# Token-major norms of a two-block transformer kernel: transposes and splits of a token tile emitted one tile later, inverse root as one GpSimd power

## The chip, the cores and the metric

One Trainium2 chip, one core. The metric is the device time of one execution in microseconds (us), median of the runs shown. Engine names are those of the profile: PE (TensorE matmul), PEld (its weight load), DVE (VectorE), ACT (ScalarE), POOL (GpSimd), SP (the engine that issues most loads).

## The reference, cut to what matters

Two transformer blocks in float32 on 512 tokens of width 1024. The change touches only the places where a sum goes into the residual stream, is normalised there and is normalised again for the next matrix product. In the second block that is, for each of two layers and three sublayers (mixers, cross attention, MLP):

```python
x = x + rms_norm(merged @ w_mix_out[l], ln_mix_post[l])
h = rms_norm(x, ln_xa_pre[l])          # goes into the next projection
```

with `rms_norm(x, g) = x * rsqrt(mean(x * x) + 1e-6) * g` over the 1024 features of a token. The end of the first block has one such place with no sum in front (`rmsnorm(x, norm_final)`), and the last sublayer writes the output and has no second norm. So there are seven such places, of which six are followed by a further projection.

## The kernel before, in words

Matrix products run as three products each: a matrix is split in a high part (ACT copies it, rounding to a shorter format) and a low part (DVE takes the difference), and PE adds hi x hi, hi x lo and lo x hi (lines 370 to 372, and 946 to 948 in the token-major form). Weights come by DMA from SP into `wraw` (3 buffers), ACT makes `whi` (L360), DVE `wlo` (L361), 3 buffers each.

`post` (lines 973 to 1057) does one of the seven places. Its product is token-major: 128 tokens on the partitions, 1024 output features in two halves m = 0 and 1, four token tiles t = 0 to 3. `wide` (L950) runs one half: the first chunks of the weights for all four tiles, and then, tile by tile, the held chunks (three of them in the second half; two in the MLP, whose last group has only two), after which it calls `done(t)`. `done` scales the sum by the gain or adds it to what is there (DVE, L1002, L1004 or L1006) and lets ACT square it with a running sum (L1008). In the second half `done(t)` goes on to `norm(t)`:

- the inverse root on DVE, ten instructions of one column each: add the two halves and epsilon (L1015), three for the start value (L1016 to L1018), three Newton steps of two (L1020, L1021);
- the update of the residual x, 128x1024 (L1024; or L1026; or L1029 and L1030);
- if a projection follows, eight PE transposes of the new x into two PSUM buffers `pax` (L1038), eight splits of their 128 columns into `hhi` (ACT, L408) and `hlo` (DVE, L409), and two ACT squares of x for the next norm (L1043).

The ten small values stand in `tss`, one buffer. The scratch output of each ACT square is a buffer of tag `dt` (six buffers, used all over the kernel, also for `vm` below).

Behind the two halves come, in order of emission: `fill` (four of the six places: four 512 KB matrices of the memory's keys or values, split, multiplied with 256 memory rows into PSUM, scaled by DVE into `vm`, L903, transposed or not, and sent out by a DMA from the POOL queue), `hold` (the first three weight tiles of the next projection), and in the next function `lead`: three output tiles of the next projection, their 512 tokens in two halves of 256 columns, so that its first half needs only the splits of tiles 0 and 1 and its second half those of tiles 2 and 3.

Order: no instruction is placed by hand. A planner in the compiler takes, for each engine and by its own estimate of durations, the earliest emitted instruction that it holds to be ready, and so fixes a queue for each engine; on the chip an engine goes through its queue strictly in order and waits where the estimate was wrong.

Of the kernel before, what the change touches and what calls it, by code (L numbers as in the profile page):

```python
# [10 lines left out]
F32 = mybir.dt.float32  # L11
F32R = mybir.dt.float32r
I32 = mybir.dt.int32
AF = mybir.ActivationFunctionType
OP = mybir.AluOpType
AX = mybir.AxisListType

P = 128
# [55 lines left out]
class Packed:  # L74
    def __init__(self):
        self.parts, self.at, self.n = [], {}, 0
# [176 lines left out]
class Kern:  # L253
    def __init__(self, ctx, tc, a, vat):
        self.tc, self.nc, self.a, self.vat = tc, tc.nc, a, vat
        pool = lambda name, bufs, **k: ctx.enter_context(tc.tile_pool(name=name, bufs=bufs, **k))
        self.const = pool("const", 1)
        self.big = pool("big", 1)
        self.wp = pool("wp", 3)
        self.wk = pool("wk", 2)  # L260
        self.ps = pool("ps", 1, space=bass.MemoryType.PSUM)
        self.turn, self.dtags, self.led, self.held = 0, ("pmm", "pr"), [], []
        self.dram = pool("dram", 2, space=bass.MemoryType.DRAM)
        nc = self.nc
        self.x = self.bigt("x", F32, "rbig")
        self.cst = self.const.tile([P, _CONST.n], F32, name="cst")
        self.vec = self.const.tile([P, a["vec"].shape[1]], F32, name="vec")
        nv = vat["norm_mix0"][1]
        nc.scalar.dma_start(self.vec[:, :nv], a["vec"][:, :nv])
        one = self.const.tile([P, 1], F32, name="one")  # L270
        nc.vector.memset(one, 0.0)
        nc.scalar.activation(one, one, AF.Exp)
        first = self.leads("pool_in")
        raws = self.half("w01", F32).rearrange("p k t -> p (k t)").rearrange("p (c k m) -> p c k m", c=2, k=KD)
        raws = [raws[:, 0], raws[:, 1], self.wtile("wraw")]
        self.held = [(self.wtile("whi"), self.wtile("wlo")) for _ in range(3)]

        def xload(ks):
            for k in ks:
                nc.sync.dma_start(self.x[:, k], a["xT"][:, k])  # L280

        xload([0])
        for part, then in ((slice(0, 4), (1, 2, 3)), (slice(4, 8), (4, 5, 6, 7))):
            for raw, ap, (hi, lo) in zip(raws, first, self.held):
                nc.sync.dma_start(raw[:, part], ap[:, part])
                nc.scalar.activation(hi[:, part], raw[:, part], AF.Copy)
                nc.vector.tensor_sub(lo[:, part], raw[:, part], hi[:, part])
            xload(then)
        nc.sync.dma_start(self.cst, a["cst"])
        nc.sync.dma_start(self.vec[:, nv:], a["vec"][:, nv:])  # L290
        self.load_phase(_CONST1, a["cst1"])
        self.ident = self.c("ident")
        self.ones = self.c("ones")[:, 0:1]
        self.nsplit = 0
# [678 lines left out]
    def post(self, chunks, xh, xl, mode, y, gname, nxt, then=(), out=None, fill=None):  # L973

        nc = self.nc
        if fill:
            fill = self.mem_kv(*fill, ("pmm", "pr"))
        g = self.rows(gname)  # L980
        old, own = self.x, mode == "own"
        if own:
            self.x = self.bigt("x", F32, "rbig")
        x = self.x
        ss = self.wk.tile([P, 4, 8], F32, name="tss", bufs=1)
        z = [None]
        pn = None
        flat = lambda v, t: v[:, 2 * t:2 * t + 2].rearrange("p m t -> p (m t)")

        def residual(m):  # L990
            def add(t, ps):
                for j in range(4):
                    nc.tensor.matmul(ps[:, j * P:(j + 1) * P], old[:, 4 * m + j, t * P:(t + 1) * P], self.ident,
                                     start=False, stop=False)
            return add if own else None

        def half(m):
            def done(t, ps):
                i = 2 * t + m
                src = ps  # L1000
                if mode == "fresh":
                    nc.vector.tensor_mul(y[:, i], ps, g[:, m * T:(m + 1) * T])  # L1002
                elif own:
                    nc.vector.tensor_copy(x[:, i], ps)  # L1004
                else:
                    nc.vector.tensor_add(y[:, i], y[:, i], ps)  # L1006
                    src = y[:, i]
                nc.scalar.activation(self.dt("sq"), src, AF.Square, scale=1.0 / 32, accum_out=ss[:, t, m:m + 1])  # L1008
                if m:
                    norm(t)  # L1010
            return done

        def norm(t):
            v, i, r, h, w = (ss[:, t, j:j + 1] for j in range(2, 7))
            nc.vector.tensor_scalar(v, ss[:, t, 0:1], ss[:, t, 1:2], 1e-6, op0=OP.add, op1=OP.add)  # L1015
            nc.vector.tensor_scalar(i.bitcast(I32), v.bitcast(I32), 1, None, op0=OP.logical_shift_right)  # L1016
            nc.vector.tensor_scalar(r.bitcast(I32), i.bitcast(I32), -1.0, float(0x5F3759DF), op0=OP.mult, op1=OP.add)
            nc.vector.tensor_scalar(h, v, -0.5, None, op0=OP.mult)  # L1018
            for _ in range(3):
                nc.vector.scalar_tensor_tensor(w, r, h, r, op0=OP.mult, op1=OP.mult)  # L1020
                nc.vector.scalar_tensor_tensor(r, w, 1.5, r, op0=OP.add, op1=OP.mult)  # L1021
            xt = flat(x, t)
            if mode == "fresh":
                nc.vector.scalar_tensor_tensor(xt, flat(y, t), r, xt, op0=OP.mult, op1=OP.add)  # L1024
            elif own:
                nc.vector.scalar_tensor_tensor(xt, xt, r, g, op0=OP.mult, op1=OP.mult)  # L1026
            else:
                yt = flat(y, t)
                nc.vector.scalar_tensor_tensor(yt, yt, r, g, op0=OP.mult, op1=OP.mult)  # L1029
                nc.vector.tensor_add(xt, xt, yt)  # L1030
            if out is not None:
                nc.sync.dma_start(out[:, 2 * t:2 * t + 2], x[:, 2 * t:2 * t + 2])
                return
            c = slice(t * P, (t + 1) * P)
            for m in range(2):
                pt = self.pax()
                for j in range(4):
                    nc.tensor.transpose(pt[:, j * P:(j + 1) * P], x[:, 2 * t + m, j * P:(j + 1) * P], self.ident)  # L1038
                for j in range(4):
                    k = 4 * m + j  # L1040
                    self.split(pn["hi"][:, k, c], pn["lo"][:, k, c], pt[:, j * P:(j + 1) * P], scale=self.v(nxt, k))
            for m in range(2):
                nc.scalar.activation(self.dt("sq"), x[:, 2 * t + m], AF.Square, accum_out=sx[:, 2 * t + m:2 * t + m + 1])  # L1043

        sx = self.wk.tile([P, 8], F32, name="tsx", bufs=1)
        self.wide(chunks[0], xh, xl, 1, half(0), residual(0))
        if nxt:
            pn = {"hi": self.bigt("hhi"), "lo": self.bigt("hlo"), "g": nxt}
        self.wide(chunks[1], xh, xl, min(3, len(chunks[1])), half(1), residual(1))
        if fill:  # L1050
            fill()
        self.hold(then)
        if nxt:
            s4 = self.wk.tile([P, 4], F32, name="ts4", bufs=1)
            nc.vector.tensor_add(s4, sx[:, 0:8:2], sx[:, 1:8:2])
            pn["st"] = {"acc": [z, z], "ps": {0: s4, 1: s4}, "r": None}
        return pn
# [756 lines left out]
```

## Time and profile before

| what | us |
|---|---|
| median of 3 runs | 3443.78 |
| the 3 runs | 3444.88, 3434.6, 3443.78 |
| the profiled execution's own time | 3447.86 |
| its span | 3446.1 |
| PE busy in it | 3334.7 |
| DVE busy | 1833.2 |
| ACT busy | 1169.0 |
| POOL busy | 262.9 |

The span is the time from the first to the last instruction of the profiled execution. Granted clock is the share of TensorE's full clock that the chip let through, 0.983 over the whole execution. In the views of single instructions, `[6.89 <-DVE x L1030]` says that the engine stood idle for 6.89 us before the instruction and what ended the wait.

The seven places lie at about 1150 to 1210 us (end of the first block), 1740 to 1812 (mixers, layer 0), 1870 to 1952 (cross attention 0), 2240 to 2335 (MLP 0), 2880 to 2950 (mixers 1), 3030 to 3095 (cross attention 1) and 3380 to 3446 us (MLP 1, the output). The second, the third, the fourth and the fifth carry a `fill`.

### The profile page before, as it was taken

The numbers are of one execution on the slowest core, as the hardware profiler recorded it, in microseconds if no ns is written. First come the engines' busy times: TensorE is split into PE (matmuls) and PEld (weight loads), VectorE is DVE, ScalarE is ACT, GpSimd is POOL, SyncE is SP. The second block draws the span as 40 slices with busy tenths as digits, with TensorE's granted clock in tenths as the row PEclk, the third lists the DMA queues.
The fourth block names the chain that finished last, engine by engine and source line by source line (L and its number), as shares of the span: only waits on it lengthen the run. The fifth ranks groups of instructions, "written<-read, shape, count | busy, mean of one in ns | idle before, by whom it ended". The sixth has DMA issues, their size and how long they took to land.

```text
span 3446.1 us, 42433 instructions
## 1 busy us (share of the span) xinstructions
PE 3334.7 (97%) x16702; PEld 2704.5 (78%) x16702; DVE 1833.2 (53%) x3521; ACT 1169.0 (34%) x2076; POOL 262.9 (8%) x229
## 2 busy tenths in 40 slices
PE   7999999999999989999999999989999999899998
PEld 6888888878888867777887888877776788778886
DVE  7554444445545466556465644466565545454445
ACT  4332232543222333322343433343342234344232
POOL 3200022001000010001200000001100121000000
PEclk9999999989999999999999999989999999999999
DMA  3323335232232231232242322223222233213222
GB/s 134 107 95 97 100 121 159 80 130 101 98 98 92 92 100 44 69 108 90 92 141 80 123 98 98 96 90 109 57 56 93 80 98 122 99 56 109 98 96 76
DMA packets 96328, 334.16 MB, mean 97 GB/s; under 512 B 12472, under 2 KB 14016, under 8 KB 93824
## 3 DMA queue, kind: packets, MB, share of 16 engines
q1 hardware_dynamic: 88912, 295.64, 26.4%
q10 hardware_dynamic: 4528, 27.15, 2.2%
q0 software_dynamic: 2688, 8.66, 1.1%
q8 instruction: 131, 2.15, 0.3%
q14 instruction: 69, 0.57, 0.1%
HBM read 311.20 MB, written 13.90 MB: 94 GB/s over the span
## 4 chain that ended last, share of the span: by engine, by line
PE 66%; DVE 7%; ACT 2%; issue 1%; POOL 0%; DMA 0%; DVEq 0%; ACTq 0%; POOLq 0%
PE pmm L372 8%; PE pmm L371 7%; PE pmm L370 7%; PE pr L372 5%; PE pr L370 5%; PE pr L371 5%; PE pr L946 3%; PE pr L947 3%; PE pr L948 3%; PE pmm L947 3%; PE pmm L946 3%; PE pmm L948 3%; DVE wlo L361 1%; PE pax L1504 1%; PE pr L1722 1%
## 5 line engine op out<-in xcount | busy, mean ns | idle before, releaser
L360 ACT ACTIVATE whi<-wraw 128x1024 fp32r<-128x1024 f32 (+2 forms) x529 | 551.1, 1044 | 1624.0 <-PE pmm L371 532.4
L361 DVE TENSOR_TENSOR wlo<-wraw,whi 128x1024 fp32r<-128x1024 f32 (+2 forms) x529 | 648.9, 1228 | 321.2 <-ACT whi L360 317.1
L372 PE MATMUL pmm<-hhi,wlo 128*128 128x512 f32 (+1 forms) x1568 | 608.3, 388 | 9.0 <-DVE wlo L361 9.0
L370 PE MATMUL pmm<-hhi,whi 128*128 128x512 f32 (+1 forms) x1568 | 609.5, 389 | 6.6 <-ACT whi L360 6.0
L371 PE MATMUL pmm<-hlo,whi 128*128 128x512 f32 (+1 forms) x1568 | 609.9, 389 | 0.9 <-DVE hlo L409 0.9
L370 PE MATMUL pr<-hhi,whi 128*128 128x512 f32 (+1 forms) x1104 | 419.5, 380 | 10.8 <-ACT hhi L408 10.4
L372 PE MATMUL pr<-hhi,wlo 128*128 128x512 f32 (+1 forms) x1104 | 417.7, 379 | 2.8 <-DVE wlo L361 2.8
L371 PE MATMUL pr<-hlo,whi 128*128 128x512 f32 (+1 forms) x1104 | 418.0, 379 | 0.9 <-DVE hlo L409 0.8
L372 PEld LDWEIGHTS pmm<-hhi,wlo 128*128 128x128 f32 x1568 | 298.9, 191 | 69.2 <-DVE wlo L361 15.7
L370 PEld LDWEIGHTS pmm<-hhi,whi 128*128 128x128 f32 x1568 | 298.3, 190 | 66.1 <-ACT whi L360 10.4
L371 PEld LDWEIGHTS pmm<-hlo,whi 128*128 128x128 f32 x1568 | 298.3, 190 | 59.6 <-issue 4.4
L370 PEld LDWEIGHTS pr<-hhi,whi 128*128 128x128 f32 x1104 | 209.8, 190 | 51.1 <-ACT hhi L408 10.8
L372 PEld LDWEIGHTS pr<-hhi,wlo 128*128 128x128 f32 x1104 | 209.4, 190 | 43.9 <-DVE wlo L361 6.7
L371 PEld LDWEIGHTS pr<-hlo,whi 128*128 128x128 f32 x1104 | 209.9, 190 | 39.7 <-DVE hlo L409 2.0
L1630 POOL TENSOR_TENSOR macc<-macc,g 128x512 f32<-128x512 f32 x48 | 71.6, 1494 | 345.7 <-DVE g L1629 236.7
L582 DVE TENSOR_TENSOR u<-pmm,rstd 128x512 f32<-128x512 f32 x44 | 30.4, 691 | 108.6 <-PE pmm L372 102.9
L577 DVE TENSOR_TENSOR g<-pr,rstd 128x512 f32<-128x512 f32 x44 | 30.4, 691 | 90.4 <-PE pr L372 89.6
L1618 DVE TENSOR_TENSOR g<-pmm,rstd 128x512 f32<-128x512 f32 x44 | 30.3, 689 | 87.2 <-PE pmm L372 87.2
L948 PE MATMUL pr<-wlo,ahl 128*128 128x512 f32 x192 | 74.8, 390 | 0.0
L946 PE MATMUL pr<-whi,ahl 128*128 128x512 f32 x192 | 74.8, 389 | 0.0
L948 PE MATMUL pmm<-wlo,ahl 128*128 128x512 f32 x192 | 74.8, 389 | 0.0
L947 PE MATMUL pmm<-whi,ahl 128*128 128x512 f32 x192 | 74.7, 389 | 0.0
(553 smaller groups left out, 5644.8 us busy)
## 6 DMA issues: line engine op xcount, KB each, us to landing
wraw<-mlp SPq DMA_DIRECT2D x128, 512.0 KB, 3.3
wraw<-w_in SPq DMA_DIRECT2D x116, 512.0 KB, 3.3
wraw<-ffn_g SPq DMA_DIRECT2D x44, 512.0 KB, 3.3
wraw<-ffn_u SPq DMA_DIRECT2D x44, 512.0 KB, 3.3
wraw<-wkv SPq DMA_DIRECT2D x32, 512.0 KB, 3.3
wraw<-qkv SPq DMA_DIRECT2D x24, 512.0 KB, 3.6
wraw<-ffn_d SPq DMA_DIRECT2D x24, 448.0 KB, 3.3
wraw<-ffn_d SPq DMA_DIRECT2D x16, 512.0 KB, 3.5
```

The lines of the kernel that those rows point to most:

```text
L360: nc.scalar.activation(hi[:, :kt, :m], raw[:, :kt, :m], AF.Copy)
L361: nc.vector.tensor_sub(lo[:, :kt, :m], raw[:, :kt, :m], hi[:, :kt, :m])
L370: nc.tensor.matmul(ps[:, cols], hi[:, i], xh[:, k, cols], start=a, stop=False)
L371: nc.tensor.matmul(ps[:, cols], hi[:, i], xl[:, k, cols], start=False, stop=False)
L372: nc.tensor.matmul(ps[:, cols], lo[:, i], xh[:, k, cols], start=False, stop=z)
L577: nc.vector.tensor_mul(g, pg, r)
L946: nc.tensor.matmul(ps, xh[:, k, c], hi[:, m], start=a, stop=False)
L947: nc.tensor.matmul(ps, xl[:, k, c], hi[:, m], start=False, stop=False)
L948: nc.tensor.matmul(ps, xh[:, k, c], lo[:, m], start=False, stop=z)
L1504: nc.tensor.matmul(poA[:, oc], eT[:, b * P:(b + 1) * P], vn[:, b * P + 64 * br:b * P + 64 * br + 64], start=b == 0, stop=b == qb)
L1630: nc.gpsimd.tensor_add(acc[:, n], acc[:, n], g)
L1722: nc.tensor.matmul(po, V[:, b, n * P:(n + 1) * P], eT[b], start=b == 0, stop=b == 1)
```

## The change

The norm is cut into `update(t)` and `feed(t)`. `feed(t - 1)`, the transposes, splits and squares, is emitted behind `update(t)`, and `feed(3)` behind `fill`. The ten DVE instructions of the inverse root go; in their place POOL adds epsilon to the first half's sum (in the first half, off the norm's chain), and then, per tile, adds the second half's sum and raises it to the power -0.5, which it reads from a one-column constant.

```diff
+        self.neghalf = self.const.tile([P, 1], F32, name="neghalf")
+        nc.vector.memset(self.neghalf, -0.5)
...
                 nc.scalar.activation(self.dt("sq"), src, AF.Square, scale=1.0 / 32, accum_out=ss[:, t, m:m + 1])
-                if m:
-                    norm(t)
+                if not m:
+                    nc.gpsimd.tensor_scalar(ss[:, t, 2:3], ss[:, t, 0:1], 1e-6, None, op0=OP.add)
+                    return
+                update(t)
+                if nxt and t:
+                    feed(t - 1)
             return done
 
-        def norm(t):
-            v, i, r, h, w = (ss[:, t, j:j + 1] for j in range(2, 7))
-            nc.vector.tensor_scalar(v, ss[:, t, 0:1], ss[:, t, 1:2], 1e-6, op0=OP.add, op1=OP.add)
-            nc.vector.tensor_scalar(i.bitcast(I32), v.bitcast(I32), 1, None, op0=OP.logical_shift_right)
-            nc.vector.tensor_scalar(r.bitcast(I32), i.bitcast(I32), -1.0, float(0x5F3759DF), op0=OP.mult, op1=OP.add)
-            nc.vector.tensor_scalar(h, v, -0.5, None, op0=OP.mult)
-            for _ in range(3):
-                nc.vector.scalar_tensor_tensor(w, r, h, r, op0=OP.mult, op1=OP.mult)
-                nc.vector.scalar_tensor_tensor(r, w, 1.5, r, op0=OP.add, op1=OP.mult)
+        def update(t):
+            r = ss[:, t, 3:4]
+            nc.gpsimd.tensor_add(ss[:, t, 4:5], ss[:, t, 1:2], ss[:, t, 2:3])
+            nc.gpsimd.tensor_tensor(r, ss[:, t, 4:5], self.neghalf, op=OP.pow)
             xt = flat(x, t)
...
             if out is not None:
                 nc.sync.dma_start(out[:, 2 * t:2 * t + 2], x[:, 2 * t:2 * t + 2])
-                return
+
+        def feed(t):
             c = slice(t * P, (t + 1) * P)
...
         if fill:
             fill()
+        if nxt:
+            feed(3)
         self.hold(then)
```

## Rows read from the trace of the kernel before

**Rows 1.** The page, busy time: engine, us (share of the span), weight loads, instructions.

```profile
PE 3334.7 (97%) x16702; PEld 2704.5 (78%) x16702; DVE 1833.2 (53%) x3521; ACT 1169.0 (34%) x2076; POOL 262.9 (8%) x229
```

**Rows 2.** Who PE waited for, whole span: us in total, times, longest.

```profile
PE pax L1038 <- DVE x L1024: 13.0, 5, 6.0
PE pmm L372 <- DVE wlo L361: 12.2, 14, 2.3
...
PE pax L1038 <- DVE x L1030: 8.9, 3, 6.9
...
PE pax L1038 <- DVE z L1104: 3.0, 1, 3.0
PE pr L370 <- ACT sq L1008: 2.6, 2, 1.4
```

**Rows 3.** Busy by stretch: PE, PEld, DVE, ACT, POOL, granted clock, DMA, GB/s.

```profile
1190.00:1210.00 20.00, 15.84 (x108) 14.57 (x106) 15.09 (x56) 11.07 (x33) 0.00 (x0) 0.91 0.50 185
1795.00:1810.00 15.00, 12.23 (x89) 10.61 (x88) 10.63 (x31) 8.98 (x27) 1.31 (x3) 1.00 0.55 195
1940.00:1950.00 10.00, 7.69 (x57) 6.67 (x56) 9.28 (x30) 7.74 (x25) 1.29 (x3) 1.00 0.32 102
2295.00:2335.00 40.00, 28.26 (x164) 25.23 (x163) 30.01 (x91) 21.50 (x61) 2.06 (x3) 0.74 0.41 148
2925.00:2950.00 25.00, 15.80 (x108) 14.50 (x107) 18.09 (x62) 13.95 (x37) 2.00 (x3) 0.80 0.40 134
3075.00:3095.00 20.00, 16.13 (x115) 15.20 (x115) 14.20 (x58) 10.14 (x31) 0.00 (x0) 0.91 0.26 80
3430.00:3446.00 16.00, 1.87 (x9) 1.22 (x7) 11.84 (x38) 1.45 (x4) 0.00 (x0) 0.63 0.32 132
```

**Rows 4.** Single instructions of MLP 0, tiles 2 and 3: start, length, engine, line.

```profile
2297.22 0.68 DVE L1006 TENSOR_TENSOR ybm<-ybm,pr 128x512 f32<-128x512 f32 x1
...
2306.91 0.39 PE L370 MATMUL pmm<-hhi,whi 128*128 128x256 f32 x1
...
2314.18 0.63 ACT L1043 ACTIVATE sq<-x 128x512 f32<-128x512 f32 x1 [3.32 <-DVE x L1030]
...
2316.73 0.63 ACT L1008 ACTIVATE sq<-ybm 128x512 f32<-128x512 f32 x1
...
2321.78 1.22 DVE L1030 TENSOR_TENSOR x<-x,ybm 128x1024 f32<-128x1024 f32 x1
2322.92 0.41 DVE L903 TENSOR_TENSOR vm<-pmm,mr 128x256 f32<-128x256 f32 x1
...
2323.06 1.97 PE L1038 MATMUL pax<-cst,x 128*128 128x128 f32 x8 [6.89 <-DVE x L1030]
```

**Rows 5.** Single instructions of mixers 0, tile 0, from sum to transposes.

```profile
1774.38 0.21 DVE L1015 TENSOR_SCALAR tss<-tss 128x1 f32<-128x1 f32 x1 [0.75 <-ACT sq L1008]
...
1776.35 1.28 DVE L1024 SCALAR_TENSOR_TENSOR x<-yb,tss,x 128x1024 f32<-128x1024 f32 x1
...
1777.69 1.09 PE L1038 MATMUL pax<-cst,x 128*128 128x128 f32 x8
```

**Rows 6.** Single lines on POOL: duration in ns, least/median/most, first and last start; one memset.

```profile
L1513 POOL TENSOR_TENSOR oC<-oC,tA x8: 728/738/1252, 1332.3 to 2579.4; 128x256 f32<-128x256 f32 x8
L1630 POOL TENSOR_TENSOR macc<-macc,g x48: 1269/1293/2366, 1550.1 to 2878.7; 128x512 f32<-128x512 f32 x48
L1805 POOL MEMSET const-float32-0.0<- 128x1 f32 x1 | 0.1, 103 | 0.2 <-issue 0.2
```

**Rows 7.** The end: the last matmul and the last update.

```profile
3431.48 0.39 PE L948 MATMUL pmm<-wlo,ahl 128*128 128x512 f32 x1
...
3440.90 1.22 DVE L1030 TENSOR_TENSOR x<-x,ybm 128x1024 f32<-128x1024 f32 x1
```

**Rows 8.** Two stretches of unbroken matmuls, of 512 and of 256 columns (columns as rows 3).

```profile
1910.00:1915.00 5.00, 5.00 (x24) 4.14 (x23) 1.92 (x2) 1.08 (x2) 0.00 (x0) 1.00 0.31 105
1815.00:1820.00 5.00, 5.00 (x44) 5.00 (x43) 0.00 (x0) 0.00 (x0) 0.00 (x0) 1.00 0.00 1
```

## The prediction

> **What bounds the kernel now.** The first view is the page's busy time: PE is busy for 3334.7 of 3446.1 us [rows 1], so the end is set by PE and no cut on another engine counts unless it takes away PE's idle time, which is 111.4 us in all. The second is the list of waits of PE: its largest single cause is the transposes L1038 waiting for the residual x: 13.0 us on L1024, 8.9 on L1030, and 3.0 put down to a DVE memset that stands behind the last x update of the first block [rows 2]. That is 24.9 us in nine waits. The third is busy time by stretch around the six places that feed a projection [rows 3]. Length minus PE busy is 4.16, 2.77, 2.31, 11.74, 9.20 and 3.87 us: 34.05 us idle. The granted clock falls there as well, to 0.91, 0.74, 0.80 and 0.91 on average in four of the six. I estimate what that costs as (1 - clock) x PE busy: 1.4 + 7.3 + 3.2 + 1.5 = 13.4 us. So the change can touch some 47 us on PE, and besides that the tail, in which PE is done at 3431.9 and the core needs 14.2 us more [rows 7].
>
> Why x comes late is in the view of single instructions. In MLP 0 the sum of tile 3 is complete at 2297.9 (L1006), but its square on ACT (L1008) starts at 2316.7, 18.8 us later; it stands in ACT's queue behind both L1043 squares of tile 2, which had to wait for tile 2's x [rows 4]. So the tiles go one behind the other: x of a tile, its squares, only then the sum of squares of the next. DVE takes the first `vm` of the fill (L903) only at 2322.9, directly behind tile 3's x, and PE stood idle for 6.89 us until then [rows 4]. Both fit the order of emission: in the old code the squares of x(t) come ahead of the square of tile t+1, and tile 3's ahead of all `vm`, and they all draw on the six `dt` buffers. The planner does move work (the lead's L370 runs at 2306.9, ahead of the transposes of tile 2 that were emitted before it), but it did not move these.
>
> **The change part by part.**
>
> *Emission one tile later.* L1008 of tile t+1 now stands ahead of the squares, transposes and splits of tile t, so the tiles' updates no longer wait for each other's feed; the fill's `vm` stands ahead of feed(3). No instruction is added or removed here: 192 transposes, 192 pairs of splits and 48 squares remain. Their cover: a tile's held chunks are 18 matmuls, at 5.00/24 = 0.21 us each 3.8 us [rows 8]. From the last matmul of tile t, x needs 0.69 + 0.8 (sum, square and its read-out), the root, and 1.28 us for L1024 [rows 5]; with a root of 1 us this is 3.8 us, just under the next tile's held chunks. For tile 3 nothing of its own product follows, but the first half of the lead does, 3 tiles x 8 x 3 = 72 matmuls of 256 columns at 5.00/44 = 0.114 us, or 8.2 us [rows 8], and with a fill another four matrices of 24 such, 10.9 us. The cover is there in all six places. What is late next: in MLP 0 the held chunks are 12 matmuls (2.5 us) and the update is two instructions (L1029, L1030), so DVE is the tighter engine: it is busy for 30.0 of 40 us in that stretch [rows 3], and `wlo` of the fill queues on DVE behind a denser burst of updates. Waits for `wlo` are already 12.2 us over the kernel [rows 2]; I leave this part in. Ends: all 34.05 us of idle goes, or none. I take three quarters, as the 24.9 us of L1038 waits are 73% of it: -25.5 us.
>
> *Clock.* The slow stretches follow the long waits (MLP 0, mixers 1) and go with them. Ends 0 and -13.4; three quarters: -10 us.
>
> *Root on POOL.* Ten DVE instructions per tile go, 1.97 us from L1015 to L1024 [rows 5], 28 times. In their place stand one add and one power in the chain, and one add off it (28 of each; POOL has no other work in these stretches but the fill's DMAs, 1.3 to 2.1 us [rows 3]). POOL's adds take 738 ns at 256 columns and 1293 at 512 [rows 6], by which a line gives 0.18 us at one column; the memset of one column took 0.10. No row shows a power. From below: two instructions at 0.18 plus two handovers, some 0.5 us. From above: the slowest POOL row, 2.37 us for each of the two, 4.7 us. I take 1.0 us, near the one-column end because the lengths scale with columns. At 1.0 the chain gets about 1 us shorter. In the six places that is no term of its own (the idle time was counted above). In the tail it is: DVE is busy for 11.84 of the last 16 us [rows 3], and the roots of tiles 1 to 3 are some 30 of its 38 instructions, while the three remaining pairs L1029, L1030 take 1.3 + 1.2 us each. I take -2.5 us; ends 0 and -4.
>
> *POOL beside DVE.* The Pool add of 128x512 takes 1269 ns at least and 2366 at most, that of 128x256 728 and 1252 [rows 6]: POOL can be held up by 0.5 to 1.1 us. If that hits each of the two root instructions, the root takes 2 to 3 us in place of 1. The Trainium skill, "SBUF — State Buffer", section "Who interferes with whom", states that a DVE instruction with two SBUF inputs and a GpSimd instruction that reads SBUF share a port pair as an exclusive lock: whichever comes second is blocked to the end of the other. The spread of these rows agrees with it. Updates and `wlo` have two SBUF inputs each, so by this rule the power waits just where DVE is dense, and the change would give less than its order promises.
>
> *New waits.* DVE's update now waits for POOL in DVE's in-order queue; behind it stand splits L409 and `wlo`. If the planner holds the power to be shorter than it is by 1 us, DVE idles up to 1 us in each of 24 tiles, of which PE feels what is not covered by its own held work; I put a quarter of that: +6 us, ends 0 and +24. The memset of the constant at the start is one DVE instruction of one column, nothing.
>
> **Sum.** -25.5 - 10 - 2.5 + 6 = -32 us. The profiled execution took 3447.86 us (span 3446.1, 1.8 around it), so 3415.9 for one like it; it lay 4.1 us above the median of the runs, and against the median of 3443.78 the sum is 3411.8, rounded to 3412.
>
> **The rivals.**
>
> *The order stays serial, only the root gets faster.* If the planner puts L1008 of the next tile late for another reason, the feed still stands between the tiles. Then only the root's share of the chain shrinks: in the four places with a fall in clock tile 3's x comes some 2 us sooner (1 us each for its own root and for that of tile 2; tiles 0 and 1 are not late), 4 x 2, less 1.5 for new waits, and the tail 2.5: -9 us, 3435. For it: the planner already reorders, and program order alone may not decide. Against it: L1008 comes late in the same position, behind both L1043 of the tile before, wherever I looked.
>
> *POOL is held up by DVE*, as in the rows above: +10 us on the forecast (a further 1 to 2 us in 24 updates, a quarter of it felt), 3422.
>
> *The power is long: slower.* The place is L1024 or L1029, waiting on DVE's queue, and the transposes that the planner has put into PE's queue for a short power. Beyond the 1.0 us that fit under a tile's 3.8 us of held work, each further us is felt by PE in each of the 24 tiles. The break-even is where 24 x (root - 1) eats the 38 us of gain: a root of 2.6 us. At the upper end, 4.7 us, the cost is 24 x 3.7 = 89 us and the sum +51; at 3.5 us, +22, or 3466. For it: no row shows this operation. Against it: two POOL instructions of one column would have to take as long as 128x512.
>
> **How the numbers follow.** The forecast as summed has 0.55, held-up POOL 0.16, the serial order 0.17, the long power 0.12. A measurement of this kernel cannot tell less than 0.3% (10.3 us) from no change, so faster means below 3433.5. The forecast is faster but for 0.02; held-up POOL for 0.02; the serial order is faster in 0.06 of its 0.17; the long power is slower in 0.08 and within 0.3% in 0.04. That makes faster 0.73, same 0.19, slower 0.08. The range goes from 3397 (all idle and three quarters of the clock and the tail, no new wait) to 3442, which takes in the serial order and leaves out the long power and the last of the lower end.
>
> **What would show it.** Right: L1008 of tiles 1 to 3 within 2 us of their sum; the nine L1038 waits down to a few us; granted clock 0.95 or more in MLP 0 and mixers 1; L903 ahead of tile 3's transposes; POOL's two instructions under 1.2 us together; the last update ending some 2 us sooner after the last matmul. Wrong: L1008 still behind L1043; new DVE idle time put down to POOL; PE waits that only changed name, to `wlo`.

## The result, and the profile after

The changed kernel takes 3389.41 us (median of four runs, 3388.32 to 3391.16) where the kernel before took 3442.15 beside it: a ratio of 0.9851, 95% interval 0.9834 to 0.9868, or 52.7 us. In a later comparison it was 3392.09 and 0.9856 (0.9842 to 0.9869). The prediction had the sign and forecast -32 us; the time lies below its range.

The page's busy time and PE's waits come first, as in [rows 1] and [rows 2].

```profile
PE 3307.5 (98%) x16702; PEld 2687.4 (79%) x16702; DVE 1788.2 (53%) x3242; ACT 1166.1 (34%) x2076; POOL 295.1 (9%) x313
```

```profile
PE pmm L374 <- DVE wlo L363: 8.0, 10, 2.3
PE pr L374 <- DVE wlo L363: 7.7, 4, 6.1
...
PE pax L1040 <- DVE hlo L411: 1.9, 2, 1.1
...
PE pax L1040 <- DVE x L1031: 1.2, 2, 0.6
```

PE's idle time is 3386.5 - 3307.5 = 79.0 us, 32.4 less than in [rows 1]. The transposes, now L1040, wait 1.2 us for x in place of 24.9, and the waits for `wlo` didn't grow in exchange (15.7 us in these two lines, 21.5 in the same two before). PE's busy time fell by 27.2 us as well, though it does the same 16702 matmuls. Some 22 us of that go with the granted clock, estimated as (1 - clock) x busy (40.3 us before, 18.1 after); 6 of these 22 lie in the first block, which the change does not touch (see below). The stretches of [rows 3], shifted so that each has the same distance from its place's last held matmul, are now (columns as there):

```profile
1184.14:1204.14 20.00, 19.79 (x159) 18.97 (x158) 12.96 (x41) 11.61 (x33) 0.74 (x2) 1.00 0.64 237
1777.65:1792.65 15.00, 14.56 (x120) 14.12 (x119) 11.23 (x34) 7.18 (x17) 1.62 (x3) 1.00 0.92 303
1919.07:1929.07 10.00, 8.93 (x72) 8.50 (x71) 7.61 (x26) 5.21 (x12) 1.08 (x2) 1.00 0.82 247
2274.74:2314.74 40.00, 36.24 (x278) 34.87 (x277) 25.26 (x62) 21.48 (x56) 5.39 (x8) 0.96 0.48 172
2883.10:2908.10 25.00, 23.21 (x189) 22.15 (x188) 16.81 (x44) 13.03 (x37) 3.54 (x6) 1.00 0.71 228
3022.91:3042.91 20.00, 19.64 (x159) 18.77 (x157) 12.26 (x39) 11.48 (x33) 0.74 (x2) 1.00 0.32 106
3372.62:3386.50 13.88, 1.87 (x9) 1.22 (x7) 8.49 (x8) 1.45 (x4) 1.68 (x4) 0.66 0.37 152
```

The last row is the tail. In the other six, the idle time is 7.6 us in place of 34.05, and the granted clock is 1.00 but for 0.96 in MLP 0. There the single instructions of tile 3, which answer to [rows 4]:

```profile
2280.52 0.68 DVE L1008 TENSOR_TENSOR ybm<-ybm,pr 128x512 f32<-128x512 f32 x1
...
2281.60 0.64 ACT L1010 ACTIVATE sq<-ybm 128x512 f32<-128x512 f32 x1
...
2285.93 1.22 DVE L1031 TENSOR_TENSOR x<-x,ybm 128x1024 f32<-128x1024 f32 x1
...
2286.72 1.05 PE L1040 MATMUL pax<-cst,x 128*128 128x128 f32 x4
...
2288.21 0.65 PE L1040 MATMUL pax<-cst,x 128*128 128x128 f32 x4
2288.48 0.41 DVE L905 TENSOR_TENSOR vm<-pmm,mr 128x256 f32<-128x256 f32 x1
```

From the end of the sum to the start of the square it is now 0.4 us, 18.8 before. The chain of mixers 0, tile 0 has the root on POOL, as against [rows 5]:

```profile
1757.19 0.19 POOL L1021 TENSOR_TENSOR tss<-tss 128x1 f32<-128x1 f32 x1 [8.69 <-ACT sq L1010]
1757.46 0.57 POOL L1022 TENSOR_TENSOR tss<-tss,neghalf 128x1 f32<-128x1 f32 x1
```

```profile
1758.07 1.28 DVE L1025 SCALAR_TENSOR_TENSOR x<-yb,tss,x 128x1024 f32<-128x1024 f32 x1 [1.74 <-POOL tss L1022]
```

It takes 0.88 us from the add to the start of the update. At the end, against [rows 7], the span ends 12.0 us behind the last matmul (14.2 before):

```profile
3374.10 0.39 PE L950 MATMUL pmm<-wlo,ahl 128*128 128x512 f32 x1
...
3381.34 1.22 DVE L1031 TENSOR_TENSOR x<-x,ybm 128x1024 f32<-128x1024 f32 x1
```

To see where the 59.6 us between the two profiled spans lie, the span is cut at landmarks that both kernels have (the first product of a place, the first matmul of `rz`, the first score). Worked out from PE's single instructions, in us, idle time in brackets:

```
stretch                                     before          after           difference
first block                                 1142.7 (25.8)   1137.1 (25.0)    -5.6
its end, up to the first rz matmul           105.6 ( 7.8)     93.9 ( 1.0)   -11.7
mixers 0, rwkv part                          493.2 (14.4)    493.2 (14.8)     0.0
mixers 0, output                             109.1 ( 2.8)    105.5 ( 0.6)    -3.5
cross attention 0, MLP 0 up                  140.1 ( 2.5)    138.8 ( 1.4)    -1.3
MLP 0, up to the next rz matmul              389.7 (15.0)    372.4 ( 5.7)   -17.3
mixers 1, rwkv part                          496.7 (15.1)    494.3 (15.2)    -2.4
mixers 1 output, cross attention 1, MLP up   250.1 (13.6)    234.5 ( 2.5)   -15.6
MLP 1                                        304.8 ( 0.0)    304.8 ( 0.0)     0.0
tail                                          14.2 (14.2)     12.0 (12.0)    -2.2
```

By these landmarks the six places (the rows 2, 4, 5, 6 and 8) and the tail give -51.6 us; the medians differ by 52.7, and by 51.2 in the later comparison. The first block's -5.6 is no effect of the change: its queues hold the same instructions in the same order in both kernels but for one memset, and in the profiled runs of all kernels below it took 1137.1 to 1142.7 us, the changed kernel itself 1137.1 once and 1142.2 once. The clock's share of it is 6.2 us ((1 - clock) x busy, 16.6 against 10.4), of which 4.6 lie at 745 to 775 us, where the granted clock was low for a longer or shorter while. The -2.4 us of mixers 1 are of this kind too: in the second profile of the changed kernel they are -0.3.

### The profile page after: what moved, and what is told of

It is laid out like the page before. It is cut to its first block, busy times and chain, and to the rows that moved or that the text cites. A ratio compares the mean times of both kernels' runs of the same rounds, so it can differ in the third digit from the quotient of the medians.

```text
span 3386.5 us, 42274 instructions
## 1 busy us (share of the span) xinstructions
PE 3307.5 (98%) x16702; PEld 2687.4 (79%) x16702; DVE 1788.2 (53%) x3242; ACT 1166.1 (34%) x2076; POOL 295.1 (9%) x313
## 4 chain that ended last, share of the span: by engine, by line
PE 66%; DVE 6%; ACT 2%; issue 1%; POOL 1%; DMA 0%; POOLq 0%; ACTq 0%; DVEq 0%; SPq 0%
PE pmm L374 8%; PE pmm L373 8%; PE pmm L372 8%; PE pr L374 5%; PE pr L372 5%; PE pr L373 5%; PE pmm L949 2%; PE pr L949 2%; PE pmm L950 2%; PE pr L948 2%; PE pr L950 2%; PE pmm L948 2%; DVE wlo L363 1%; PE pax L1508 1%; PE pr L1726 1%
## 5 line engine op out<-in xcount | busy, mean ns | idle before, releaser
L372 PEld LDWEIGHTS pr<-hhi,whi 128*128 128x128 f32 x1104 | 208.4, 189 | 49.4 <-ACT hhi L410 10.1
L373 PEld LDWEIGHTS pr<-hlo,whi 128*128 128x128 f32 x1104 | 208.4, 189 | 38.4 <-DVE hlo L411 1.1
L1012 POOL TENSOR_SCALAR tss<-tss 128x1 f32<-128x1 f32 x28 | 8.7, 309 | 1256.9 <-ACT sq L1010 1256.9
L410 ACT ACTIVATE hhi<-pax,vec 128x128 fp32r<-128x128 f32 x192 | 62.1, 371 | 42.4 <-PE pax L1040 22.5
```

What stands on the lines that cost most here:

```text
L372: nc.tensor.matmul(ps[:, cols], hi[:, i], xh[:, k, cols], start=a, stop=False)
L373: nc.tensor.matmul(ps[:, cols], hi[:, i], xl[:, k, cols], start=False, stop=False)
L410: nc.scalar.activation(hi, src, AF.Copy, scale=scale)
```

## The experiments

All times are medians; the kernel before took 3442.7 to 3443.7 us beside them.

**Only the order** (the root stays ten DVE instructions):

```diff
-                if m:
-                    norm(t)
+                if not m:
+                    return
+                update(t)
+                if nxt and t:
+                    feed(t - 1)
...
+        if nxt:
+            feed(3)
```

> Only the order: update(t) and feed(t - 1) as in the change, feed(3) behind the fill, but the ten DVE instructions of the inverse root stay. Theory (the order carries the gain, the root is small): 3392 to 3405 us, that is 37 to 50 of the 53 us; the tail stays at about 14 us behind the last matmul, and waits of PE on x in MLP 0 come back with 1 us each at most, because the root takes 1.97 us in place of 1.0. Rival (the root carries it: 28 x 1.97 = 55 us of DVE go, about the whole gain): 3433 to 3445. Rival (only both together, DVE too dense with the root on it): 3405 to 3425.

Measured 3405.33 us, ratio 0.9894 (0.9879 to 0.9909): -38.4, where the theory's range ends and that of the second rival begins. By the landmarks the six places give -36.2 us and the tail nothing: it is 14.2 us, as before. In MLP 0 one wait of PE stays, on the x of tile 2, and it is 6.38 us where I expected 1 at most. The root of that tile was drawn out to 8.67 us (DVE, from its first instruction, here L1018, to the update):

```profile
2283.46 0.21 DVE L1018 TENSOR_SCALAR tss<-tss 128x1 f32<-128x1 f32 x1
...
2292.13 1.28 DVE L1032 SCALAR_TENSOR_TENSOR ybm<-ybm,tss,gr 128x1024 f32<-128x1024 f32 x1
...
2294.85 1.97 PE L1042 MATMUL pax<-cst,x 128*128 128x128 f32 x8 [6.38 <-DVE x L1033]
```

**Only the root** (the old order; add and power on POOL, `norm(t)` with transposes and splits behind its own update):

```diff
+                if not m:
+                    nc.gpsimd.tensor_scalar(ss[:, t, 2:3], ss[:, t, 0:1], 1e-6, None, op0=OP.add)
+                    return
+                norm(t)
...
+            nc.gpsimd.tensor_add(ss[:, t, 4:5], ss[:, t, 1:2], ss[:, t, 2:3])
+            nc.gpsimd.tensor_tensor(r, ss[:, t, 4:5], self.neghalf, op=OP.pow)
```

> Only the root: add and power on POOL in place of ten DVE instructions, transposes and splits emitted directly behind the update of their tile as before. Theory (order carries it): the tiles still go one behind the other, each link 1 us shorter, some 1 us in each of up to 8 late tiles and 2 in the tail: 3428 to 3438. Rival (root carries it): 3388 to 3400. If the two parts add up, root_only and order_only together save 53 us; if each removes the same wait, their savings add up to more than 53, and if they need each other, to less.

Measured 3403.97 us, ratio 0.989 (0.9876 to 0.9905): -39.8. My theory falls: the root alone is worth as much as the order alone. The two savings sum to 78 us, the change gives 51 to 53, so each takes away much of the same waits. And this though the order stays serial: in mixers 0 both squares L1042 of tile 0's x still stand ahead of tile 1's L1010. But they are done before the sum of tile 1 is, and L1010 waits for that sum alone:

```profile
1764.38 0.63 ACT L1042 ACTIVATE sq<-x 128x512 f32<-128x512 f32 x1 [2.35 <-DVE x L1023]
...
1765.01 0.62 ACT L1042 ACTIVATE sq<-x 128x512 f32<-128x512 f32 x1
...
1767.31 0.60 ACT L1010 ACTIVATE sq<-pr 128x512 f32<-128x512 f32 x1 [0.29 <-DVE yb L1004]
```

In the kernel before, the square of tile 3 in the same place stands 11.6 us behind its sum:

```profile
1788.12 0.68 DVE L1002 TENSOR_TENSOR yb<-pr,gr 128x512 f32<-128x512 f32 x1
...
1800.36 0.60 ACT L1008 ACTIVATE sq<-pr 128x512 f32<-128x512 f32 x1
```

The same distance, from the end of a tile's sum in the second half to the start of its square, for tiles 0 to 3 (us, worked out from single instructions):

```
kernel            mixers 0                MLP 0
before            0.0  1.2  4.4  11.6     0.0  4.7  13.5  18.8
root_only         0.0  0.1  0.1   0.1     0.0  2.9   5.7   7.6
one_newton        0.0  0.1  1.0   0.7     0.0  2.9  13.2  17.0
order_only        0.0  0.0  0.4   0.1     0.0  0.0   1.1   0.8
squares_later     0.0  0.0  0.1   0.2     0.0  0.0   1.1   2.2
changed           0.0  0.0  0.1   0.4     0.0  0.0   0.1   0.4
```

(one_newton and squares_later are runs further down.) In the old order with the long root the delay grows from tile to tile. The new order takes the link away; a shorter root leaves the link, but in five of the six places the delay no longer builds up (root_only: 0.8 us at most there). Only in MLP 0, where a tile has 12 held matmuls in place of 18, does it stay. So both cuts remove much the same delay, and their savings don't add.

What I had not looked at is how long the old root really took. In MLP 0 of the kernel before, DVE's queue for tile 1 reads:

```profile
2296.26 0.21 DVE L1015 TENSOR_SCALAR tss<-tss 128x1 f32<-128x1 f32 x1 [0.26 <-ACT sq L1008]
...
2297.81 0.21 DVE L1020 SCALAR_TENSOR_TENSOR tss<-tss 128x1 f32<-128x1 f32 x1
2297.97 0.61 DVE L409 SCALAR_TENSOR_TENSOR hlo<-pax,vec,hhi 128x128 fp32r<-128x128 f32 x2
2298.50 0.15 DVE L1021 SCALAR_TENSOR_TENSOR tss<-tss 128x1 f32<-128x1 f32 x1
2298.57 1.22 DVE L361 TENSOR_TENSOR wlo<-wraw,whi 128x1024 fp32r<-128x1024 f32 x1
...
2300.22 0.21 DVE L1020 SCALAR_TENSOR_TENSOR tss<-tss 128x1 f32<-128x1 f32 x1
2300.35 1.22 DVE L361 TENSOR_TENSOR wlo<-wraw,whi 128x1024 fp32r<-128x1024 f32 x1
2301.48 0.15 DVE L1021 SCALAR_TENSOR_TENSOR tss<-tss 128x1 f32<-128x1 f32 x1
2301.55 1.22 DVE L361 TENSOR_TENSOR wlo<-wraw,whi 128x1024 fp32r<-128x1024 f32 x1
...
2303.13 1.28 DVE L1029 SCALAR_TENSOR_TENSOR ybm<-ybm,tss,gr 128x1024 f32<-128x1024 f32 x1
```

Between its one-column instructions, each of which needs the one before, the planner had put three `wlo`, six splits and a sum. The root took 6.87 us from L1015 to the update. Over the 28 tiles this is 99.8 us, 3.57 on average (two expectations below give 3.3; there the last two tiles of the output were paired with the update of the tile before); only tile 0 of five places has the 1.97 us of [rows 5], and tiles 1 to 3 of the six places average 4.0. The POOL root takes 25.7 us in 28, 0.92 each.

**Only the squares L1043 one tile later** (from the kernel before, nothing else):

```diff
-            for m in range(2):
-                nc.scalar.activation(self.dt("sq"), x[:, 2 * t + m], AF.Square, accum_out=...)
+            if t:
+                squares(t - 1)
...
+        if nxt:
+            squares(3)
```

> The kernel before with one thing moved: the two squares L1043 of tile t are emitted one tile later (those of tile 3 behind the fill); transposes, splits and the root on DVE stay in place. Theory (the sum of squares of the next tile stood behind these two squares in ACT's queue, and they behind x): 3392 to 3412, nearly that of the order alone. Rival (the transposes and splits of the tile, eight hhi on ACT and eight hlo on DVE, keep the next tile's sum and update back as well): 3425 to 3442.

Measured 3403.18 us, ratio 0.9888 (0.9873 to 0.9903): -40.6, no worse than the whole order. So what the new order cures is the place of these squares in ACT's queue: in mixers 0, tile 1's square now stands ahead of tile 0's L1043 squares (here L1047).

```profile
1773.41 0.60 ACT L1008 ACTIVATE sq<-pr 128x512 f32<-128x512 f32 x1 [3.93 <-DVE yb L1002]
1774.49 0.64 ACT L1047 ACTIVATE sq<-x 128x512 f32<-128x512 f32 x1
```

Whether the planner had kept the old order for the order of emission alone or also for the six `dt` buffers is not shown by any run.

The DVE root got longer in this run, 5.33 us on average from its first instruction to the update (3.57 before, 4.00 in order_only), and the kernel is 40 us faster all the same. So the length of the root is not a price by itself: it costs where the next tile waits for it, as in the old order.

**feed(3) ahead of the fill**, otherwise the changed kernel:

```diff
-        if fill:
-            fill()
         if nxt:
             feed(3)
+        if fill:
+            fill()
```

> The changed kernel, but the transposes and splits of tile 3 are emitted ahead of the fill. Theory (the fill was held back by x of tile 3 only because the chain of updates was late; with the chain early the place of feed(3) matters little): 3388 to 3397. Rival (vm ahead of feed(3) is what keeps PE busy in the four places with a fill): 2 to 6 us in each, 3397 to 3413.

Measured 3403.74 us, ratio 0.9883 (0.9866 to 0.9899). The theory falls, the rival holds: the place behind the fill is worth 12 to 14 us by the medians. By the landmarks it is 10.5 in the six places, 9 of them in MLP 0; the rest of the difference lies in stretches that the edit does not touch. In MLP 0 the first `vm` starts 16.7 us after the last held matmul, 12.2 in the changed kernel and 26.4 before. The update of tile 3 ends at the same distance in both new kernels, 10.9 us.

**The old order, root on POOL made longer:**

```diff
+            for _ in range(10):
+                nc.gpsimd.tensor_scalar(r, r, 1.0, None, op0=OP.mult)
```

> The old order with the root on POOL, made longer by ten POOL multiplications by 1.0 in the chain (0.27 us each from start to start, as add and power stand 0.27 apart): a root of some 3.6 us in place of 0.9, near the 3.3 us that the DVE root took from its first instruction to the update, mean over its 28 tiles, in the kernel before. DVE stays free of the ten instructions. Theory (what counts is the time from the sum of squares to the update, which the interleaving of ten dependent instructions with wlo and splits had drawn out): 3430 to 3448, the whole gain of root_only is lost. Rival (what counts is that DVE has 28 x 1.97 us less to do): 3398 to 3412.

Measured 3487.37 us, ratio 1.0129 (1.0115 to 1.0143). The root took 3.8 us in most tiles and 4.7 in several last ones. That DVE has less to do does not carry the gain by itself: with DVE's ten instructions gone and the root long, the kernel is 45 us slower than before. It costs more than I expected, 83 us over the short root for 3.0 us more per tile, about 28 us per us. DVE pays it by standing still, in all 89.5 us before its three kinds of update (28.4 in root_only):

```profile
DVE x L1025 <- POOL tss L1022: 51.4, 16, 4.7
DVE ybm L1030 <- POOL tss L1022: 25.1, 8, 4.7
DVE x L1027 <- POOL tss L1022: 13.0, 4, 4.7
```

**The old order, both roots** (the short POOL root is used; DVE's ten instructions run as well, into columns that nobody reads):

> The old order with the root on POOL, and the ten DVE instructions as well, whose result nobody reads. DVE's load is that of the kernel before, the chain is the short one. Theory (the chain counts): 3400 to 3412, as root_only, the dead instructions costing at most a few us where they stand ahead of an update in DVE's queue. Rival (DVE's load counts): 3432 to 3447.

Measured 3419.73 us, ratio 0.9932 (0.992 to 0.9945), between the two expectations: 23 of root_only's 40 us stay, 17 go with DVE's instructions back in the queue. The update waits behind them in tile 3 (1.9 to 3.2 us from POOL's add to the update in four places, 0.86 in most other tiles), so part of the 17 is chain again. How much is load alone was not separated.

**The old order, one Newton step in place of three**, all on DVE (a less exact root):

```diff
-            for _ in range(3):
+            for _ in range(1):
```

> The kernel before with one Newton step in place of three, all on DVE in the old order: six dependent instructions in place of ten (the two steps left out make the root less exact). Theory (the gain of a short root is that DVE's dependent instructions, between which wlo and splits are put, are fewer; POOL is not needed for it): the root's mean of 3.3 us falls to about 2, and the time by about half of root_only's 40 us, 3414 to 3430. Rival (POOL is what helps, by working beside DVE): 3434 to 3444.

Measured 3419.17 us, ratio 0.9932 (0.992 to 0.9945): -24 with four instructions of ten gone and no POOL. The median from L1015 to the update fell from 3.4 to 2.2 us; the mean fell from 3.57 to 2.77, drawn up by tile 3 of two places (8.3 and 9.3 us, four `wlo` between its six instructions in the first of them, two of which waited for `whi`). POOL is one way to a shorter root, not the only one. DVE has less to do here as well, so this run does not part the chain from the load.

**The changed kernel with a longer root**, eight and twenty extra POOL instructions (same edit as above):

> The changed kernel with eight POOL multiplications by 1.0 behind the power: a root of some 3.1 us, above the break-even of 2.6 us that the prediction's rival of a long power gave. Theory (with the new order the updates don't wait for one another, so a longer root shows only behind tile 3 and in the tail): +2 in the tail and 1 to 3 in each of four or five places, 3394 to 3406. Rival of the prediction (24 us per us of root): 3435 to 3446.

> The changed kernel with twenty such multiplications: a root of some 6.3 us, longer than the 3.8 us of a tile's held matmuls, so that POOL itself falls behind by 2.5 us per tile. Theory: tile 3's update 13 us later in each of six places, of which the lead and the fill cover 8 to 19, and 10 in the tail: 3410 to 3450. Rival of the prediction (24 us per us): 3500 or more.

Measured 3451.88 us, ratio 1.0032 (1.0021 to 1.0043), with a root of 3.2 us in most tiles, and 3541.45 us, ratio 1.0284 (1.027 to 1.0298), with one of 6.7 where POOL was free (7.5 on average). My theory, that the new order would hide a longer root, falls twice, and the rival of the prediction holds nearly to the number: (3451.88 - 3392.09) / 2.3 = 26 us per us of root from 0.9 to 3.2, and 89.6 / 3.5 = 26 beyond. The price is as high on the first stretch as on the second, so on average little beyond 0.9 us is hidden, and no run has a shorter root that would show whether the 0.9 are. By a straight line between the two runs the break-even is 0.9 + 51.2 / 26 = 2.9 us; the prediction said 24 per us and 2.6. DVE in mixers 0 shows the way it goes, between tiles 2 and 3 of the kernel with eight:

```profile
1779.20 0.61 DVE L411 SCALAR_TENSOR_TENSOR hlo<-pax,vec,hhi 128x128 fp32r<-128x128 f32 x2 [0.56 <-ACT hhi L410]
1782.20 1.29 DVE L1027 SCALAR_TENSOR_TENSOR x<-yb,tss,x 128x1024 f32<-128x1024 f32 x1 [2.39 <-POOL tss L1024]
...
1783.93 1.22 DVE L363 TENSOR_TENSOR wlo<-wraw,whi 128x1024 fp32r<-128x1024 f32 x1
```

The update stands at the head of DVE's queue for 2.39 us, and the splits and `wlo` that PE needs stand behind it. Over the kernel DVE waits 79.7 us for the root (29.3 in the changed kernel), and PE's transposes wait for x again:

```profile
PE pax L1042 <- DVE x L1027: 19.7, 12, 3.3
```

**The same with eight, feed two tiles later:**

```diff
-                if nxt and t:
-                    feed(t - 1)
+                if nxt and t > 1:
+                    feed(t - 2)
...
+        if nxt:
+            feed(2)
         if fill:
             fill()
```

> root_plus8 (root of 3.2 us on POOL, new order) with the transposes and splits of a tile emitted two tiles later in place of one (those of tile 2 ahead of the fill, of tile 3 behind it). Theory (the price of a long root is PE's transposes, put into its queue for the short POOL instructions that the planner counts on, and PE waits there with the next tile's matmuls behind them): most of the 50 us on x goes, and 8 in the tail and the delay of tile 3 stay, 3400 to 3425. Rival (the price is in the chain of tile 3 and in what hangs on it): 3440 to 3455.

Measured 3458.03 us, ratio 1.0047 (1.0035 to 1.006), 6 us slower than root_plus8. PE's waits for x fell from 28.5 us to 4.5 in two waits, but the time only changed name:

```profile
PE pax L1042 <- DVE hlo L411: 21.5, 5, 6.4
PE pmm L372 <- ACT whi L362: 16.4, 11, 3.1
PE pmm L374 <- DVE wlo L363: 15.1, 15, 2.5
```

DVE still waits 88.6 us for the root. So the place of the transposes in PE's queue is not the price. That it is DVE's standing still fits all four kernels with a long root (137.8 us in the one with twenty). No run took that standing away with the root left long, so this is read from the rows and not isolated.

**All eight squares L1043 behind feed(3) and the hold**, meant as a better version:

> The changed kernel with all eight squares L1043 (the sum for the next norm) emitted behind feed(3) and the hold, as nothing near needs them. It is meant to beat both kernels. Theory (ACT's hhi and whi come sooner; the six places still hold some 11 us of idle time): 3383 to 3389, 0 to 6 us under the changed kernel. Rival (the squares collide with the lead's whi and with the sum that the next rstd needs): 3390 to 3398.

Measured 3399.78 us, ratio 0.9875 (0.9862 to 0.9889), some 8 us slower than the changed kernel beside it. By the landmarks 5 us are lost at the end of the first block and 2 in MLP 0. A miss. The rival fits, that the moved squares meet the lead's `whi` on the same engine; which instruction pays was not isolated.

**The changed kernel once more:**

> The changed kernel once more, beside the others on one chip: 3386 to 3392 us. Its first block, whose queues are those of the kernel before instruction by instruction, takes 1137 to 1143 us, whatever comes behind it.

Measured 3392.09 us, as said above. No kernel tried here beats it.

## Why the prediction was right in kind and wrong in size

- *What bounds the kernel* held. The end moved by PE's idle time and clock in the six places, and by the tail.
- *Emission one tile later, -25.5 us of idle time, and clock, -10 us.* The mechanism held: L1010 of tile 3 stands 0.4 us behind its sum, and the single move of the squares shows that ACT's queue was the link. The sizes held as well. The test of these two terms is order_only, which has the new order and the old root: by the landmarks the idle time of the six places went from 41.7 to 19.9 us, -21.8, and the clock's cost ((1 - clock) x busy in stretches of 5 us) from 14.5 to 6.1, -8.4. With another 6 us of PE's busy time, which neither idle time nor granted clock accounts for and which stay open, that is -36.2, where the two terms had -35.5. So near a hit is in part luck: both terms were too large, and the 6 us made up for it. In the changed kernel, with the short root too, 11.2 us of idle time and 1.7 of clock are left.
- *Where the idle time lay.* I counted it only in the windows of [rows 3], 34.05 us; by the landmarks the places held 41.7. Outside my windows lay, among others, two waits for `wlo` in the stretch of the next projection (kernel before, single instructions and stretches; columns as in [rows 3]):

```profile
1222.28 0.68 PE L372 MATMUL pmm<-hhi,wlo 128*128 128x512 f32 x1 [2.27 <-DVE wlo L361]
...
2354.27 0.50 PE L372 MATMUL pr<-hhi,wlo 128*128 128x512 f32 x1 [2.25 <-DVE wlo L361]
```

```profile
1220.00:1225.00 5.00, 2.73 (x8) 2.14 (x8) 4.07 (x8) 0.00 (x0) 1.88 (x1) 0.74 0.32 102
2355.00:2360.00 5.00, 5.00 (x16) 3.95 (x16) 3.03 (x4) 0.00 (x0) 0.12 (x1) 0.66 0.66 215
```

  Both are gone in the changed kernel, with the falls in clock beside them. That tile 3 came late, and that what hung on it pushed the next `wlo` back, is my reading and not isolated: in order_only the first of the two is still there, with 1.94 us.
- *Root on POOL: the step that failed.* "At 1.0 the chain gets about 1 us shorter. In the six places that is no term of its own". The 1.0 us was right (0.92 measured), the old root was not: I took 1.97 us from mixers 0, tile 0, where nothing else was ready for DVE, and multiplied it by 28. On average it was 3.57 us and in tiles 1 to 3 4.0, because `wlo` and splits stood between its instructions. So I put the root at nothing in the six places. Put on top of the new order it gave 13.2 us there: the places give -49.4 us in the changed kernel and -36.2 in order_only, about 8 of the difference in idle time and 4.4 in clock. For the same reason I priced the rival in which it alone helps at 9 us, with two late tiles a place and 1 us each, where the run showed 40: each root was 2.5 us shorter on average (1.03 in place of 3.57), and the delay that grew from tile to tile no longer built up.
- *Tail, -2.5 us:* -2.2, and the order alone gives none of it.
- *New waits, +6 us:* DVE does stand 29.3 us for POOL in the changed kernel, but PE's list shows only 1.2 us of waits for x. As far as the rows show, the term was near 0, its lower end.
- *POOL beside DVE.* One root add took 1.14 us in place of 0.19, while a `wlo` ran (changed kernel, MLP 0, tile 3):

```profile
2282.28 1.22 DVE L363 TENSOR_TENSOR wlo<-wraw,whi 128x1024 fp32r<-128x1024 f32 x1
2282.40 1.14 POOL L1021 TENSOR_TENSOR tss<-tss 128x1 f32<-128x1 f32 x1 [5.55 <-ACT sq L1010]
```

  It ends at 2283.54, 0.04 us after the `wlo`. That is as the Trainium skill says in "SBUF — State Buffer", section "Who interferes with whom": the second of the two waits until the first is done. Three root adds of 24 in the six places met such an instruction, two of them for 0.2 us only; all roots there but this one (1.80 us) took 0.85 to 1.03 us, so this rival did not decide.
- *What would show it:* the squares, the waits, the clock, POOL's length (but for the one root above) and the tail came as written. `vm` ahead of tile 3's transposes came in mixers 0 (5.9 us against 7.3 after the last held matmul) but not in MLP 0 (12.2 against 10.5 and 12.0); its earlier emission is nevertheless worth the 10.5 to 14 us of feed3_first.

In sum, in us, forecast and measured: the order with its clock -35.5 and -36.2, the root in the six places 0 and -13.2, the tail -2.5 and -2.2, new waits +6 and none that the rows show; together -32 and -51.6.

## What to carry to other kernels

Where tiles hang on one another, price a chain of small dependent instructions by the time from its first to whoever waits for its last, in every place where it runs; the one undisturbed copy of it was about half of that here (1.97 us against 3.57), since a planner puts long work between its instructions. Where the tiles don't hang on one another, the same chain can be longer and cost less, as in squares_later. Two cuts at the same delay do not add: each alone gave 38 and 40 us here, both together 51 to 53. And a wait that is moved to another engine was cheap only while it was short: at 0.9 us PE's list showed 1.2 us of waits for x, and each further microsecond cost 26. By the rows that is an engine that goes through its queue in order and stands still with all that others need behind it.

## What the runs showed of the hardware

A POOL power of one column takes 0.55 us and an add 0.19, 0.27 from the start of the add to the start of the power that needs it. In the changed kernel six of the 28 root adds came while DVE ran an instruction with both inputs in SBUF (`wlo` or the sum into x); each ended 0.05 us after that instruction, with 0.29 to 1.14 us. Beside a split, which reads one of its two matrices from PSUM, adds kept their 0.19 us. The first block, with the same queues, took between 1137 and 1143 us in the profiled runs, with the granted clock low for a longer or shorter while at 745 to 775 us: differences of 5 us between two profiled spans can come from a stretch that no edit touched.
